# FFN of a two-layer encoder: gate and up as 2x2 blocks with seven products, down as a stretch of its own

## The chip, the cores and the metric

The kernel runs on one core of a Trainium2 chip. The metric is device microseconds of one launch. PE is TensorE's matmul engine and PEld its weight load, DVE is VectorE, ACT is ScalarE, POOL is GpSimd, SP is SyncE, which issues most DMAs. A bank is one of the eight PSUM banks of 128 x 512 f32.

## The reference

Two layers over 1024 tokens of 1024 features, everything in f32. The change touches the third line of a layer:

```
x = x + w_out( concat_g RMSNorm_g(out_g) )      # mixing: attention, gating, conv
h = RMSNorm(x);  gu = h @ w_gate_up             # 1024 -> 2 x 2816
x = x + (silu(gate) * up) @ w_down              # 2816 -> 1024
x = x + (p @ w_ple_proj) * sigmoid(RMSNorm(x) @ w_ple_gate)   # "PLE"
```

`D_FF` is 2816, so gate and up have 22 feature tiles of 128 each. RMSNorm's factor per token can be put in after a product, since it scales a whole token.

## The kernel before

Tokens stand on the free axis. The 1024 tokens are two halves of 512 (`hf` 0 and 1), the features eight tiles of 128 (`m`). A product of one 128 x 128 weight tile with 512 tokens is three matmuls (`step_mm`, L220 to L224): weights and tokens are each split into a rounded part and its remainder, high by high, high by low and low by high. The rounded part is a copy on ACT (`copy_h`), the remainder a subtraction on DVE (`sub_l`). `load_w` loads 128 x 1024 weights (512 KB) and splits them with one such copy (`wh`) and one subtraction (`wl`).

After mixing, `wo_first` and `wo_second(hf)` add w_out's product to X; `norm_add` makes the split form `hl` of X times the gain and sums its square on ACT and POOL; `norm_end` makes the factor per token (a power on POOL, L265) and spreads it (`bc`). Half 0 is ready earlier than half 1, since attention of the second half still runs as a background job (`bg.tick`), so the FFN begins with feature tiles 0 to 3 on half 0 alone (AHEAD, BEHIND) and gives half 1 its share of them at the end.

`gate_up(fi)` makes eight products for gate and eight for up of each half, the evacuation multiplying by `bc` (L1114), silu on ACT (L1115), another factor on POOL (L1116), gate times up on DVE (L1121), and then the split form `act` (L123, L126). `down(fs, acts)` takes the split activations of two feature tiles, for each of the eight output tiles and each half, and adds the bank into X on DVE (L1140). It runs one group behind gate and up (`pend`, `flush`), so a bank is evacuated while the next products run. After the last group `norm_add` forms the PLE's `hl`, and `ple(hf)` follows.

The code is written in this order, and a scheduler of the framework, working from its own times, fixes at build time the order of the instructions of each engine. Each engine then takes its queue strictly in that order; semaphores do the rest. Split forms live in 38 buffers of 4 KB (`U`), temporaries in six (`T`), weights in three buffers each of `raw`, `wh` and `wl`, PSUM in pools of three (`BA`), four (`BT`) and one bank (`BO`).

Of the kernel before, what the change touches and what calls it, by code (L numbers as in the profile page):

```python
# [12 lines left out]
ALU = mybir.AluOpType  # L13
# [59 lines left out]
def tile_encoder_trunk(ctx: ExitStack, tc: tile.TileContext, x, p, positions, norm_mix_g, w_in,  # L73
# [128 lines left out]


# [252 lines left out]
    for layer in range(DEPTH):  # L456
# [622 lines left out]
        def wo_second(hf):  # L1079
            xps = [U("X").rearrange("p (m s) -> p m s", m=2) for _ in range(4)]  # L1080
            for mp in range(4):
                nc.scalar.dma_start(out=xps[mp], in_=xd[2 * mp:2 * mp + 2, :, HALF[hf]]
                                    .rearrange("m p s -> p m s"))
            for mp in range(4):
# [3 lines left out]
                for m in (2 * mp, 2 * mp + 1):  # L1088
# [7 lines left out]
                    norm_add(nrm[hf], xo, "ffn", layer)  # L1096
# [3 lines left out]
        nx = [None, None]  # L1100

        def gate_up(fi, halves, bank, eng):
            acts, s = {}, {}

            def ff_unit(c0, evac):
                wh, wl = load_w(rows_of(w_gate_up[layer], 0, NK, c0, P), (NK, P), eng, eng and nc.vector)
                for hf in halves:
                    half_mm(bank, [((wh[:, k, :], wl[:, k, :]), nrm[hf].hl[k]) for k in range(NK)],
                            lambda b: evac(hf, b))

            def ev_gate(hf, b):
                t = s[hf] = T("sg")
                bc = nrm[hf].bc
                nc.vector.tensor_tensor(out=t, in0=b, in1=bc, op=ALU.mult)  # L1114
                nc.scalar.activation(t, t, AF.Silu)  # L1115
                nc.gpsimd.tensor_tensor(out=t, in0=t, in1=bc, op=ALU.mult)  # L1116

            def ev_up(hf, b):
                t = s[hf]
                a = acts[hf] = U("act", F32R)  # L1120
                nc.vector.tensor_tensor(out=t, in0=b, in1=t, op=ALU.mult)  # L1121
                copy_h(a[:, 0:512], t)
                sub_l(a[:, 512:1024], t, a[:, 0:512])

            ff_unit(fi * P, ev_gate)
            ff_unit(DFF + fi * P, ev_up)
            return acts

        def down(fs, acts, halves, bank, eng, last):
            ws = [load_w(rows_of(w_down[layer], fi * P, 1, 0, D), (1, D), eng, eng and nc.vector)  # L1130
                  for fi in fs]
            for hf in last:
                nx[hf] = Norm()
            for m in range(NK):
                cs = slice(m * P, (m + 1) * P)
                for hf in halves:
                    xo = X[hf][m]

                    def ev(b):
                        nc.vector.tensor_tensor(out=xo, in0=b, in1=xo, op=ALU.add)  # L1140

                    half_mm(bank, [((wh[:, 0, cs], wl[:, 0, cs]), a[hf])
                                   for (wh, wl), a in zip(ws, acts)], ev)
                    if hf in last:
                        norm_add(nx[hf], xo, "ple", layer)

        pend = []

        def ffn(fs, halves, bank=BU, eng=None, last=()):
            acts = [gate_up(fi, halves, bank, eng) for fi in fs]  # L1150
            flush()
            pend.append((fs, acts, halves, bank, eng, last))
# [133 lines left out]
```

## Time and profile before

| | us |
|---|---|
| median of 3 runs | 2527.86 (2526.82 to 2532.4) |
| the profiled execution | 2526.26 |
| its span | 2524.5 |
| PE busy | 2419.4 |
| DVE busy | 1367.7 |
| ACT busy | 799.9 |
| POOL busy | 572.4 |

The span is what the profile shows of one execution; 1.76 us of the profiled execution lie outside of it. The granted clock, averaged over the span, was 0.984 of full speed. The windows 500 to 1100 us and 1750 to 2300 us lie within the two layers' FFNs; a layer's PLE begins behind 1157 us and 2400 us. A row's last part in square brackets is the time that the engine stood idle before the instruction, and what released it.

### The profile page before, as it was taken

How to read it: one execution, taken by the hardware profiler on the slowest of the kernel's cores; microseconds unless marked ns; L12 is line 12 of the kernel's file. 1: busy time of each engine (PE TensorE's matmuls, PEld its weight loads, DVE VectorE, ACT ScalarE, POOL GpSimd, SP SyncE). 2: the span in 40 equal slices, each digit the busy share in tenths (PEclk: the TensorE clock that was granted, in tenths of full speed). 3: DMA queues.
4: the chain of work that ended last, by engine and by line, in shares of the span. 5: the costliest groups of instructions: out<-in, count | busy, mean ns of one | idle time of the engine just before them, and what ended most of it. 6: DMA issues, size and time to landing. Idle time of an engine off the chain costs nothing. (4 is left out here: it accounts for less than half of the span.)

```text
span 2524.5 us, 29666 instructions
## 1 busy us (share of the span) xinstructions
PE 2419.4 (96%) x11932; PEld 2034.0 (81%) x11932; DVE 1367.7 (54%) x2111; ACT 799.9 (32%) x1392; POOL 572.4 (23%) x423
## 2 busy tenths in 40 slices
PE   8898989999999999999999898899999999999999
PEld 6797767888888888887889876678888888888877
DVE  6996676534434434466469666764433443435652
ACT  5246573221111111135423456613111111112432
POOL 4123417410000000023421233363100000001321
PEclk9898999999999999999999899999999999999999
DMA  6110512311111111124321122132111111112232
GB/s 212 30 52 14 173 34 80 113 59 50 43 50 51 50 50 43 59 75 130 113 63 39 34 90 94 58 109 76 58 43 50 50 51 50 42 51 67 84 113 71
DMA packets 210538, 175.19 MB, mean 69 GB/s; under 512 B 5940, under 2 KB 191888, under 8 KB 210400
## 3 DMA queue, kind: packets, MB, share of 16 engines
q1 hardware_dynamic: 203904, 163.60, 21.0%
q10 hardware_dynamic: 6016, 9.45, 1.1%
q8 instruction: 94, 1.54, 0.2%
q0 software_dynamic: 480, 0.24, 0.1%
q14 instruction: 44, 0.36, 0.0%
HBM read 152.29 MB, written 20.97 MB: 69 GB/s over the span
## 5 line engine op out<-in xcount | busy, mean ns | idle before, releaser
L123 ACT ACTIVATE wh<-raw 128x1024 fp32r<-128x1024 f32 x198 | 208.1, 1059 | 810.4 <-PE pa L223 451.2
L222 PE MATMUL pa<-hl,wh 128*128 128x512 f32 x1128 | 443.3, 395 | 7.8 <-ACT hl L123 4.5
L224 PE MATMUL pa<-hl,wl 128*128 128x512 f32 x1128 | 442.3, 392 | 2.7 <-POOL wl L214 2.5
L223 PE MATMUL pa<-hl,wh 128*128 128x512 f32 x1128 | 443.4, 393 | 1.0 <-DVE hl L129 0.8
L1116 POOL TENSOR_TENSOR sg<-sg,st 128x512 f32<-128x512 f32 x88 | 138.6, 1576 | 1090.0 <-ACT sg L1115 1090.0
L214 DVE TENSOR_TENSOR wl<-raw,wh 128x1024 fp32r<-128x1024 f32 x198 | 249.0, 1265 | 60.5 <-ACT wh L123 59.0
L224 PE MATMUL pt<-hl,wl 128*128 128x512 f32 x664 | 259.7, 391 | 4.4 <-DVE wl L214 4.4
L222 PE MATMUL pt<-hl,wh 128*128 128x512 f32 x664 | 259.5, 391 | 0.0
L223 PE MATMUL pt<-hl,wh 128*128 128x512 f32 x664 | 259.0, 390 | 0.0
L222 PEld LDWEIGHTS pa<-hl,wh 128*128 128x128 f32 x1128 | 213.3, 189 | 54.0 <-ACT hl L123 6.5
L224 PEld LDWEIGHTS pa<-hl,wl 128*128 128x128 f32 x1128 | 213.6, 189 | 48.0 <-POOL wl L214 2.8
L223 PEld LDWEIGHTS pa<-hl,wh 128*128 128x128 f32 x1128 | 213.8, 190 | 45.9 <-DVE hl L129 2.2
L1140 DVE TENSOR_TENSOR X<-pa,X 128x512 f32<-128x512 f32 x226 | 155.0, 690 | 110.9 <-PE pa L224 109.8
L602 PE MATMUL pa<-wh,hl 128*128 128x256 f32 x640 | 180.8, 288 | 16.4 <-ACT zkv L615 11.7
L604 PE MATMUL pa<-wl,hl 128*128 128x256 f32 x640 | 182.3, 287 | 0.7 <-DVE wl L214 0.7
L605 PE MATMUL pa<-wh,hl 128*128 128x256 f32 x640 | 181.3, 286 | 0.0
L222 PE MATMUL pa<-act,wh 128*128 128x512 f32 x426 | 166.2, 390 | 1.3 <-DVE X L1140 1.3
L223 PE MATMUL pa<-act,wh 128*128 128x512 f32 x426 | 165.8, 389 | 0.0
L224 PE MATMUL pa<-act,wl 128*128 128x512 f32 x426 | 165.3, 390 | 0.0
L259 POOL TENSOR_TENSOR st<-st,sq 128x512 f32<-128x512 f32 x82 | 122.4, 1493 | 155.6 <-ACT sq L258 130.0
L488 DVE SCALAR_TENSOR_TENSOR acc<-glu,cols,acc 128x1009 f32<-128x1009 f32 (+14 forms) x120 | 154.2, 1287 | 1.3
L224 PEld LDWEIGHTS pt<-hl,wl 128*128 128x128 f32 x664 | 125.0, 188 | 30.8 <-DVE wl L214 4.9
(273 smaller groups left out, 4353.5 us busy)
## 6 DMA issues: line engine op xcount, KB each, us to landing
raw<-in_w_gate_up_dram SPq DMA_DIRECT2D x104, 512.0 KB, 3.9
raw<-in_w_down_dram SPq DMA_DIRECT2D x52, 512.0 KB, 3.7
raw<-in_w_ple_gate_dram SPq DMA_DIRECT2D x32, 512.0 KB, 4.4
raw<-in_w_in_dram SPq DMA_DIRECT2D x28, 512.0 KB, 3.8
raw<-in_w_out_dram SPq DMA_DIRECT2D x24, 512.0 KB, 3.6
xr<-xd SPq DMA_DIRECT2D x16, 512.0 KB, 3.3
xd<-xr SPq DMA_DIRECT2D x16, 512.0 KB, 2.6
X<-xd ACTq DMA_DIRECT2D x16, 512.0 KB, 5.1
```

The costliest lines, as they stand in the source:

```text
L123: nc.scalar.activation(dst, src, AF.Copy, scale=scale)
L214: (eng or nc.vector).tensor_tensor(out=l, in0=raw, in1=f(h), op=ALU.subtract)
L222: nc.tensor.matmul(b, lhsT=wh, rhs=hl[:, 0:512], start=first, stop=False)
L223: nc.tensor.matmul(b, lhsT=wh, rhs=hl[:, 512:1024], start=False, stop=False)
L224: nc.tensor.matmul(b, lhsT=wl, rhs=hl[:, 0:512], start=False, stop=last)
L259: (eng or nc.gpsimd).tensor_tensor(out=n.s, in0=n.s, in1=sq, op=ALU.add)
L488: nc.vector.scalar_tensor_tensor(out=a[:, lo:hi], in0=glu[c][:, lo + d:hi + d], scalar=wcol(t), in1=a[:, lo:hi], op0=ALU.mult, op1=ALU.add)
L602: nc.tensor.matmul(o, lhsT=x_[:, th], rhs=wh, start=(kc + k == 0), stop=False)
L604: nc.tensor.matmul(o, lhsT=x_[:, th], rhs=wl, start=False, stop=False)
L605: nc.tensor.matmul(o, lhsT=x_[:, tl], rhs=wh, start=False, stop=(kc == 1 and k == 3))
L1116: nc.gpsimd.tensor_tensor(out=t, in0=t, in1=bc, op=ALU.mult)
L1140: nc.vector.tensor_tensor(out=xo, in0=b, in1=xo, op=ALU.add)
```

## The change

Gate and up are computed as a product of 2 x 2 blocks: feature tiles 2j and 2j + 1 by the two halves of the features k (0 to 3 and 4 to 7) by the two halves of the tokens. Seven block products give all four result blocks where eight were made.

`first(j)` makes two of the seven: the full product of feature tile 2j with half 0, whose first four k are one of the seven and all eight of which are the result block. It reads the bank once in the middle, after k = 3 (`s1`, stored to DRAM in `sum_d`), and once at the end, for gate and for up. It uses `hl` of half 0 as before; the activation goes to DRAM (`act_d`).

`token_forms(k)` makes the five token blocks of the other products from normalised X of both halves (four scaled X, two sums each on DVE and on POOL, then `split` for each form: one ACT copy, one DVE subtraction), for each of four k.

`rest(j)` makes the other five for gate (i = 0) and then for up (i = 1), 4 k each. It reads `s1` back, loads four weight blocks, combines them on POOL in four instructions, splits five weight blocks (`wform`), and adds the products in two ways: some in one bank, some by DVE at evacuation. silu stands at the end of gate. The results go to DRAM.

Down follows as its own stretch. For each half, eight banks stay open over 22 feature tiles; for each tile its weights are loaded (so twice in all) and the activation is read back and split. X is reloaded from `xd`, to which `wo_second` stores it, and gets the eight banks at the end; `norm_add` for the PLE follows, with half 0's `norm_end` in the middle of half 1's.

The core of the diff (what the additions replace is in the listing of the kernel before):

```diff
         def wo_second(hf):
...
-                    norm_add(nrm[hf], xo, "ffn", layer)
+                    if hf == 0:
+                        norm_add(nrm[hf], xo, "ffn", layer)
+                    else:
+                        add_square(nrm[hf], xo, m)
+                nc.sync.dma_start(out=xd[2 * mp:2 * mp + 2, :, HALF[hf]]
+                                  .rearrange("m p s -> p m s"), in_=xp)
...
+        def first(j):
+            hl0, bc = nrm[0].hl, nrm[0].bc
+            c0 = 2 * j * P
+            a = None
+            for i, off in enumerate((0, DFF)):
+                wh, wl = load_w(rows_of(w_gate_up[layer], 0, NK, off + c0, P), (NK, P),
+                                nc.gpsimd if ahead else None, nc.vector if ahead else None)
+                b = BA()
+                for k in range(NK):
+                    step_mm(b, (wh[:, k, :], wl[:, k, :]), hl0[k], k == 0, k % HK == HK - 1, True)
+                    if k == HK - 1:
+                        s1 = T("s1")
+                        nc.vector.tensor_tensor(out=s1, in0=b, in1=bc, op=ALU.mult)
+                        nc.sync.dma_start(out=sum_d[j][i], in_=s1)
+                    if k % 2 == 1:
+                        bg.tick()
+                if i == 0:
+                    a = T("sg")
+                    nc.vector.tensor_tensor(out=a, in0=b, in1=bc, op=ALU.mult)
+                    nc.scalar.activation(a, a, AF.Silu)
+                    nc.gpsimd.tensor_tensor(out=a, in0=a, in1=bc, op=ALU.mult)
+                else:
+                    nc.vector.tensor_tensor(out=a, in0=b, in1=a, op=ALU.mult)
+                    nc.sync.dma_start(out=act_d[2 * j][:, HALF[0]], in_=a)
+        def split(src, eng=None):
+            hl = U("tf", F32R)
+            copy_h(hl[:, 0:512], src)
+            sub_l(hl[:, 512:1024], src, hl[:, 0:512])
+            return hl
+        def token_forms(k):
+            for hf in range(2):
+                for m in (k, k + HK):
+                    normed(hf, m)
+            b11, b21, b12, b22 = X[0][k], X[0][k + HK], X[1][k], X[1][k + HK]
+            t1 = T("t1")
+            nc.vector.tensor_tensor(out=t1, in0=b12, in1=b11, op=ALU.subtract)
+            nc.gpsimd.tensor_tensor(out=b12, in0=b22, in1=b12, op=ALU.subtract)
+            nc.vector.tensor_tensor(out=b11, in0=b22, in1=t1, op=ALU.subtract)
+            forms[0][k] = split(b11)
+            forms[1][k] = split(b12)
+            nc.gpsimd.tensor_tensor(out=b21, in0=b21, in1=b11, op=ALU.subtract)
+            forms[2][k] = split(t1)
+            forms[3][k] = split(b21)
+            forms[4][k] = split(b22)
+        def rest(j):
...
+                def wform(src):
...
+                    copy_h(h, src)
+                    sub_l(l, src, h)
+                    return h, l
...
+                def out_of(dst, src, b):
+                    if i == 0:
+                        nc.vector.tensor_tensor(out=dst, in0=b, in1=src, op=ALU.add)
+                        nc.scalar.activation(dst, dst, AF.Silu)
+                    else:
+                        c = T("cu")
+                        nc.vector.tensor_tensor(out=c, in0=b, in1=src, op=ALU.add)
+                        nc.vector.tensor_tensor(out=dst, in0=c, in1=dst, op=ALU.mult)
+                bank = BT if i else BA
+                tt(out=s3, in0=a21, in1=a22, op=ALU.add)
...
+                bb, bd, bc_ = bank(), bank(), bank()
+                prod(bb, wform(a11), 0, True, True)
+                u2, g = T("u2"), T("g")
+                nc.vector.tensor_tensor(out=u2, in0=bb, in1=s1, op=ALU.add)
+                prod(bd, wform(a21), 1, True, True)
+                nc.vector.tensor_tensor(out=g, in0=bd, in1=u2, op=ALU.add)
+                prod(bc_, wform(s3), 2, True, True)
+                out_of(gb[:, 512:1024], g, bc_)
+                prod(bd, wform(a22), 3, False, True)
+                out_of(gb[:, 0:512], u2, bd)
+                prod(bc_, wform(a12), 4, False, True)
+                out_of(ga[:, 512:1024], u2, bc_)
...
+        for j in range(AHEAD):
+            first(j)
         bg.drain()
+        first(AHEAD)
         wo_second(1)
+        for k in range(HK):
+            token_forms(k)
+        for j in range(AHEAD + 1, AHEAD + 1 + BEHIND):
+            first(j)
+        for j in range(NP2):
+            rest(j)
+            if AHEAD + 1 + BEHIND + j < NP2:
+                first(AHEAD + 1 + BEHIND + j)
...
+        for hf in range(2):
...
+            banks = [BO()] + [BA() for _ in range(3)] + [BT() for _ in range(4)]
+            for fi in range(NF):
+                wh, wl = load_w(rows_of(w_down[layer], fi * P, 1, 0, D), (1, D))
+                t = T("ac")
+                nc.sync.dma_start(out=t, in_=act_d[fi][:, HALF[hf]])
+                a = split(t)
+                for m in range(NK):
+                    cs = slice(m * P, (m + 1) * P)
+                    step_mm(banks[m], (wh[:, 0, cs], wl[:, 0, cs]), a, fi == 0, fi == NF - 1)
```

The change moves the order of the engines' queues in three places that matter below. The first is DVE in the steady part of an FFN. Before, remainders of weights (`wl`) stand among the evacuations of the two halves' gate (`sg`, L1114) and up (L1121):

```order
L1114 TENSOR_TENSOR sg_921_5743<-pa_920_5718,st_323_2467 128x512
L1114 TENSOR_TENSOR sg_923_5772<-pt_922_5747,st_324_2468 128x512
L214 TENSOR_TENSOR wl_940_5906<-raw_938_5904,wh_939_5905 128x1024
L1121 TENSOR_TENSOR sg_921_5743<-pa_927_5782,sg_921_5743 128x512
L126 TENSOR_TENSOR act_928_5807<-sg_921_5743,act_928_5807 128x512
L1121 TENSOR_TENSOR sg_923_5772<-pa_929_5811,sg_923_5772 128x512
L214 TENSOR_TENSOR wl_947_5970<-raw_945_5968,wh_946_5969 128x1024
L126 TENSOR_TENSOR act_930_5836<-sg_923_5772,act_930_5836 128x512
L1114 TENSOR_TENSOR sg_935_5871<-pt_934_5846,st_323_2467 128x512
```

Now, from the last evacuation of a gate block (`ga`, L1208) to the end of the up block's first five:

```order
L1208 TENSOR_TENSOR ga_1165_7017<-pa_1173_7032,u2_1176_7049 128x512
L125 TENSOR_TENSOR wl_1190_7134<-rw_1183_7121,wh_1189_7133 128x512 x2
L125 TENSOR_TENSOR wl_1194_7168<-ws_1185_7125,wh_1193_7167 128x512
L125 TENSOR_TENSOR wl_1194_7168<-rw_1184_7122,wh_1193_7167 128x512
L125 TENSOR_TENSOR wl_1198_7204<-rw_1184_7122,wh_1197_7203 128x512
L1224 TENSOR_TENSOR u2_1191_7149<-pt_1186_7130,s1_1182_7119 128x512
L1226 TENSOR_TENSOR g_1192_7150<-pt_1187_7131,u2_1191_7149 128x512
L1212 TENSOR_TENSOR cu_1195_7183<-pt_1188_7132,g_1192_7150 128x512
```

All of the next block's remainders stand together right behind the block's last evacuation, where before one stood among the evacuations of other products. ACT at the same place, before:

```order
L1115 ACTIVATE sg_921_5743<-sg_921_5743 128x512
L123 ACTIVATE wh_939_5905<-raw_938_5904 128x1024
L1115 ACTIVATE sg_923_5772<-sg_923_5772 128x512
L123 ACTIVATE act_928_5807<-sg_921_5743 128x512
L123 ACTIVATE wh_946_5969<-raw_945_5968 128x1024
L123 ACTIVATE act_930_5836<-sg_923_5772 128x512
```

and now:

```order
L1209 ACTIVATE gb_1166_7018<-gb_1166_7018 128x512 x2
L1209 ACTIVATE ga_1165_7017<-ga_1165_7017 128x512
L122 ACTIVATE wh_1189_7133<-rw_1183_7121 128x512 x2
L122 ACTIVATE wh_1193_7167<-ws_1185_7125 128x512
L122 ACTIVATE wh_1193_7167<-rw_1184_7122 128x512
```

The copies `wh` of the next block's first two products stand behind silu of `ga`, which waits for DVE's evacuation of `ga`; before, copies and silus alternated, and the copy stood ahead of the units that it served.

The second place is DVE where half 1 of X is done and its normalisation ends (`ms`, L263 before, then L268). Before, with the forms `hl` of half 1 and the evacuations of the first gates:

```order
L129 SCALAR_TENSOR_TENSOR hl_762_4527<-X_728_4346,cols1_145,hl_762_4527 128x512
L214 TENSOR_TENSOR wl_787_4684<-raw_785_4682,wh_786_4683 128x1024
L263 TENSOR_SCALAR ms_766_4539<-po_764_4533 128x4
L1114 TENSOR_TENSOR sg_772_4579<-pt_771_4554,st_323_2467 128x512
L214 TENSOR_TENSOR wl_794_4748<-raw_792_4746,wh_793_4747 128x1024
L1121 TENSOR_TENSOR sg_772_4579<-pa_776_4589,sg_772_4579 128x512
L126 TENSOR_TENSOR act_777_4614<-sg_772_4579,act_777_4614 128x512
L1114 TENSOR_TENSOR sg_782_4649<-pt_781_4624,st_323_2467 128x512
L1114 TENSOR_TENSOR sg_784_4678<-pa_783_4653,st_324_2468 128x512
```

Now the same place, from the last two of the eight `normed` (L1153), with the sums of `token_forms` at L1163 and L1165, the middle read `s1` of a first product at L1131, and the first remainder of a token form at L125:

```order
L1153 SCALAR_TENSOR_TENSOR X_726_4430<-X_726_4430,cols1_189,st_324_2512 128x512
L1153 SCALAR_TENSOR_TENSOR X_728_4432<-X_728_4432,cols1_189,st_324_2512 128x512
L1163 TENSOR_TENSOR t1_760_4618<-X_725_4429,X_613_3787 128x512
L1163 TENSOR_TENSOR t1_766_4642<-X_725_4429,X_613_3787 128x512
L1163 TENSOR_TENSOR t1_772_4666<-X_726_4430,X_614_3788 128x512
L1163 TENSOR_TENSOR t1_778_4690<-X_726_4430,X_614_3788 128x512
L1131 TENSOR_TENSOR s1_788_4729<-pa_787_4716,st_323_2511 128x512
L1165 TENSOR_TENSOR X_613_3787<-X_727_4431,t1_760_4618 128x512
L1165 TENSOR_TENSOR X_613_3787<-X_727_4431,t1_766_4642 128x512
L1165 TENSOR_TENSOR X_614_3788<-X_728_4432,t1_772_4666 128x512
L1165 TENSOR_TENSOR X_614_3788<-X_728_4432,t1_778_4690 128x512
L125 TENSOR_TENSOR tf_761_4622<-X_613_3787,tf_761_4622 128x512
```

Twelve instructions of the token forms (eight scaled X, four sums) stand ahead of the first product's middle read; behind it come four sums and five remainders before the end of that product (`sg`, L1137).

The third place is SP's queue of DMA issues at the end of the FFN of the first layer. Before, the last feature tiles' weights and the PLE's inputs:

```order
L209 DMA raw_1289_8500<-in_w_gate_up_dram 128x8x128
L209 DMA raw_1294_8535<-in_w_gate_up_dram 128x8x128
L209 DMA raw_1299_8570<-in_w_down_dram 128x1024
L209 DMA raw_1302_8576<-in_w_down_dram 128x1024
L1183 DMA pin_1317_8650<-in_p_dram 128x4x256
L1183 DMA pin_1320_8666<-in_p_dram 128x4x256
L209 DMA raw_1323_8682<-in_w_down_dram 128x1024
L209 DMA raw_1326_8688<-in_w_down_dram 128x1024
```

Now, where down begins (`ac` is an activation read back, `X` the reload):

```order
L1291 DMA ac_1266_7501<-act0_97 128x512
L211 DMA raw_1263_7495<-in_w_down_dram 128x1024
L1291 DMA ac_1271_7536<-act1_98 128x512
L1291 DMA ac_1276_7571<-act2_99 128x512
L1233 DMA act20_117<-ga_1200_7224 128x512
L1291 DMA ac_1281_7606<-act3_100 128x512
L1291 DMA ac_1286_7641<-act4_101 128x512
L1285 DMA X_1251_7479<-xd_96 128x2x512
L1285 DMA X_1252_7480<-xd_96 128x2x512
L1285 DMA X_1253_7481<-xd_96 128x2x512
L1285 DMA X_1254_7482<-xd_96 128x2x512
L211 DMA raw_1268_7530<-in_w_down_dram 128x1024
```

The down weights of the second feature tile are now issued behind a store of the last results (`act20`), which waits for them, five reads and four loads of X.

## Rows read from the trace of the kernel before

**Rows 1.** The page: the span, and TensorE's share of it.
```profile
span 2524.5 us, 29666 instructions
PE 2419.4 (96%) x11932; PEld 2034.0 (81%) x11932; DVE 1367.7 (54%) x2111; ACT 799.9 (32%) x1392; POOL 572.4 (23%) x423
```

**Rows 2.** Windows of the two FFNs: PE, PEld, DVE, ACT, POOL, clock, DMA.
```profile
500.00:1100.00 600.00, 600.00 (x2649) 496.82 (x2648) 250.17 (x327) 111.74 (x146) 67.37 (x43) 1.00 0.17 51
1750.00:2300.00 550.00, 550.00 (x2428) 455.43 (x2427) 221.39 (x289) 93.06 (x120) 54.03 (x35) 1.00 0.17 49
```

**Rows 3.** Timeline in the first FFN: start, duration, engine, line, operation.
```profile
701.72 0.39 PE L224 MATMUL pa<-hl,wl 128*128 128x512 f32 x1
701.95 0.39 PE L222 MATMUL pt<-hl,wh 128*128 128x512 f32 x1
702.15 0.69 DVE L1114 TENSOR_TENSOR sg<-pa,st 128x512 f32<-128x512 f32 x1 [4.75 <-PE pa L224]
702.94 0.61 ACT L1115 ACTIVATE sg<-sg 128x512 f32<-128x512 f32 x1
703.06 1.23 DVE L214 TENSOR_TENSOR wl<-raw,wh 128x1024 fp32r<-128x1024 f32 x1 [0.23 <-ACT wh L123]
...
707.39 0.39 PE L222 MATMUL pa<-hl,wh 128*128 128x512 f32 x1
```

**Rows 4.** Groups by line and shape: busy us, mean ns of one, idle before.
```profile
L126 DVE TENSOR_TENSOR act<-sg,act 128x512 fp32r<-128x512 f32 x88 | 66.7, 758 | 29.3 <-ACT act L123 29.3
L126 DVE TENSOR_TENSOR pT<-pt,pT 128x512 fp32r<-128x512 f32 x96 | 64.4, 687 | 17.3 <-ACT pT L123 16.9
L123 ACT ACTIVATE wh<-raw 128x1024 fp32r<-128x1024 f32 x198 | 208.1, 1059 | 810.4 <-PE pa L223 451.2 <-PE pt L223 288.3 <-issue 30.1
L123 ACT ACTIVATE act<-sg 128x512 fp32r<-128x512 f32 x88 | 55.6, 632 | 197.2 <-DVE sg L1121 197.2
L123 ACT ACTIVATE hl<-X,cols 128x512 fp32r<-128x512 f32 x80 | 56.9, 718 | 135.7 <-DVE X L1093 74.2 <-POOL X L1245 36.4 <-DVE X L1140 24.9
L258 ACT ACTIVATE sq<-X 128x512 f32<-128x512 f32 x70 | 43.1, 618 | 22.7 <-DVE X L1093 13.8 <-POOL as L940 6.2 <-DVE X L1140 2.7
L265 POOL TENSOR_TENSOR rcol<-ms,mhalf 128x4 f32<-128x4 f32 x12 | 14.8, 1238 | 51.5 <-DVE ms L263 51.5
L1245 POOL TENSOR_TENSOR X<-sg,X 128x512 f32<-128x512 f32 x31 | 41.3, 1334 | 95.1 <-DVE sg L1238 95.1
```

**Rows 5.** Timeline after the first FFN: DVE beside POOL, and alone.
```profile
1150.03 8.09 POOL L259 TENSOR_TENSOR st<-st,sq 128x512 f32<-128x512 f32 x5 [24.29 <-ACT st L255]
...
1152.40 4.59 DVE L129 SCALAR_TENSOR_TENSOR hl<-X,cols,hl 128x512 fp32r<-128x512 f32 x3
...
1158.11 1.40 DVE L129 SCALAR_TENSOR_TENSOR hl<-X,cols,hl 128x512 fp32r<-128x512 f32 x2
```

**Rows 6.** Timeline: three waits of PE at a layer's PLE.
```profile
1161.77 0.80 PE L224 MATMUL pt<-hl,wl 128*128 128x512 f32 x1 [4.43 <-DVE wl L214]
...
2401.73 0.50 PE L222 MATMUL pa<-pT,pwh 128*128 128x512 f32 x1 [2.40 <-ACT pwh L123]
...
2414.61 0.77 PE L222 MATMUL pa<-hl,wh 128*128 128x512 f32 x1 [2.98 <-DVE sg L1238]
```

**Rows 7.** Windows of 5 us around those waits.
```profile
1160.00:1165.00 5.00, 3.23 (x8) 2.56 (x9) 5.00 (x5) 2.15 (x3) 2.77 (x2) 0.66 0.34 101
2400.00:2405.00 5.00, 3.08 (x12) 2.25 (x13) 5.00 (x4) 3.91 (x5) 4.06 (x3) 1.00 0.10 31
2410.00:2415.00 5.00, 2.02 (x9) 1.43 (x8) 2.43 (x5) 2.11 (x2) 1.05 (x2) 0.93 0.82 227
2415.00:2420.00 5.00, 5.00 (x19) 3.95 (x19) 2.90 (x3) 1.12 (x2) 2.51 (x2) 0.73 0.61 180
```

**Rows 8.** The busiest window's DMA rate, and issues to landing of down weights.
```profile
25.00:30.00 5.00, 4.98 (x24) 3.83 (x23) 4.97 (x7) 2.31 (x5) 2.07 (x2) 1.00 1.02 394
...
raw<-in_w_down_dram SPq DMA_DIRECT2D x52, 512.0 KB, 3.7
```

More of the change, by code (lines that the diff above doesn't have):

```diff
@@ L43 @@
 N_T = 6
-FG = 2
 PLE_LAG = 2
-N_AHEAD = 4
-AHEAD = ((0, 1), (2,))
-BEHIND = ((3,),)
+NP2 = NF // 2
+AHEAD = 4
+BEHIND = 3
 C1 = 1
@@ L201, in tile_encoder_trunk @@
     xd = dp.tile([NK, P, S], F32, name="xd")
+    act_d = [dp.tile([P, S], F32, name=f"act{i}") for i in range(NF)]
+    sum_d = [[dp.tile([P, 512], F32, name=f"sum{i}_{j}") for j in range(2)] for i in range(NP2)]
     def load_w(src, shape, eng=None, heng=None):
@@ L1095, in wo_second @@
                     half_mm(BA, [((wh[:, k, cs], wl[:, k, cs]), mhl[hf][k]) for k in range(4)], ev)
-                    norm_add(nrm[hf], xo, "ffn", layer)
-            norm_end(nrm[hf])
[L1100 to L1152, printed above, removed]
-        def flush():
-            if pend:
-                a = pend.pop()
-                down(*a)
-                for hf in a[-1]:
-                    norm_end(nx[hf], BO)
+                    if hf == 0:
+                        norm_add(nrm[hf], xo, "ffn", layer)
+                    else:
+                        add_square(nrm[hf], xo, m)
@@ new lines, in tile_encoder_trunk, with normed @@
+        forms = [[None] * HK for _ in range(5)]
+        def split(src, eng=None):
[3 more added lines that the diff above has]
+            return hl
+        def normed(hf, m):
+            nc.vector.scalar_tensor_tensor(out=X[hf][m], in0=X[hf][m], scalar=col("ffn", layer, m),
+                                           in1=nrm[hf].bc, op0=ALU.mult, op1=ALU.mult)
+        def token_forms(k):
[13 more added lines that the diff above has]
+            forms[4][k] = split(b22)
@@ L1161, in tile_encoder_trunk @@
+        xpair = [None, None]
+        ahead = True
         wo_first()
@@ L1203, in tile_encoder_trunk @@
             pw.append((ph, pl))
+        nx = [None, None]
+        for hf in range(2):
+            xps = [U("X").rearrange("p (m s) -> p m s", m=2) for _ in range(4)]
+            for mp in range(4):
+                nc.sync.dma_start(out=xps[mp], in_=xd[2 * mp:2 * mp + 2, :, HALF[hf]]
+                                  .rearrange("m p s -> p m s"))
+            banks = [BO()] + [BA() for _ in range(3)] + [BT() for _ in range(4)]
[7 more added lines that the diff above has]
+                    step_mm(banks[m], (wh[:, 0, cs], wl[:, 0, cs]), a, fi == 0, fi == NF - 1)
+            nx[hf] = Norm()
+            for m in range(NK):
+                xo = X[hf][m] = xps[m // 2][:, m % 2]
+                nc.vector.tensor_tensor(out=xo, in0=banks[m], in1=xo, op=ALU.add)
+                if hf and m == 0:
+                    norm_end(nx[0], BO)
+                norm_add(nx[hf], xo, "ple", layer)
         last = layer == DEPTH - 1
@@ L1252, in ple @@
                 norm_end(nrm[hf], BO)
-        for hf in range(2):
-            ple(hf)
+        ple(0)
+        norm_end(nx[1], BO)
+        ple(1)
 _INS = ['x', 'p', 'positions', 'norm_mix_g', 'w_in', 'q_norm_g', 'k_norm_g', 'sink', 'gm_ln_g',
```

56 lines of the change are left out of this document (41 added, 15 removed).

## The prediction

> **What bounds the kernel now.** I began with the page: PE is busy 2419.4 of 2524.5 us [rows 1]. An average hides stages, so windows of the two FFNs came next: PE is busy 600.00 of 600 us and 550.00 of 550, DVE 250 and 221, at a granted clock of 1.00 (2.4 GHz) and about 50 GB/s [rows 2]. In an FFN nothing is waited for, so every matmul taken away is time gained and every new wait is time lost, in full. The timeline gives the pace: from 701.95 to 707.39 begin 24 matmuls, 5.44 us, or 0.227 each (a record's 0.39 overlaps the next one) [rows 3]. The same rows show why no evacuation is felt: PE goes on at 701.95 in another bank while DVE reads the old one at 702.15.
>
> **The matmuls.** Gate and up of a layer were 44 weight tiles x 8 k x 2 halves x 3 = 2112 matmuls. Now `first` makes 11 x 2 x 8 x 3 = 528 and `rest` 11 x 2 x 5 x 4 x 3 = 1320: 264 fewer, 59.9 us per layer, 119.7 in all. Down's count stays.
>
> **Boundaries between blocks.** Within `rest` each block's weight forms stand behind the last evacuation of the block before. From gate to up, counted from the start of the last matmul: 0.43 until DVE begins (701.72 to 702.15), evacuation 0.69, 0.10, silu 0.61 [rows 3], two copies of 512 at 0.63 [rows 4] (PE's first wait is for the second), 0.05 to PE: 3.14, less the usual 0.23, is 2.9 us. 11 of them are 32.1 per layer. From up to gate no silu stands between; PE gets four matmuls (0.91) that need copies alone, then waits for 0.43 + 0.69, the product with silu 0.69, two remainders at 0.72 (between 0.687 and 0.758 [rows 4]) and 0.05: 3.30, less the 1.13 that five matmuls take anyway, is 2.2. There are ten, of which a `first` covers three: 7 x 2.2 = 15.2. Together 47 (low 38: 2.5 and 1.5 each; high 52, if DVE is also slowed by POOL's weight sums). Within a block products in three banks cover the evacuations, 12 matmuls (2.7 us) to each, so these cost nothing; if that cover went, each of the 5 evacuations would show its 0.69. The two weight loads and the `s1` of a block are issued a block ahead (60 matmuls, 13.6 us), and POOL's four weight sums (5.3 at 1.33) end within it.
>
> **Token forms.** DVE does, in a row, 8 scaled X at 0.70 (1158.11) [rows 5], 8 sums at 0.69, 20 remainders at 0.72, 3 `wl` at 1.23 [rows 3] and 11 evacuations at 0.69: 36.9 us. The power of the normalisation adds 1.24 [rows 4]. POOL makes 8 sums of 1.33 meanwhile, 10.6 us; beside POOL a DVE instruction with two SBUF inputs took 4.59/3 = 1.53 where alone it took 0.70 [rows 5], so 0.54 us is lost per us of POOL, at most 5.8; I take 5. That is 43 us against 96 matmuls of `first`, 21.8 us: PE idles 21 (15, if half 1's early part hides behind w_out; 28, if POOL's power comes late). The Trainium skill ("SBUF — State Buffer", section "Who interferes with whom") says that such a DVE instruction and a reading GpSimd one exclude each other for a whole instruction; by it the loss would be up to 10.6 and the idle time 27; the rows agree in kind but show half the loss.
>
> **The smaller terms, per layer.** Ahead of the attention's end, the second product's middle read stands behind 8 scaled X of half 0 (5.6), a weight copy (1.2 by the DVE row of 1024) and two evacuations (1.4); 12 matmuls (2.7) cover: 5.5, and `bc` 1.5 late: 7 (4 if background work fills PE; 13 if the scaled X run beside POOL at 1.53). The three `first` among the `rest` have their middle read behind a gate evacuation, 1.6 each (0.43 + 2 x 0.69 - 0.23): 4.8 (0; 6). Where down starts, ACT has pT 0.63, two PLE weights and one down weight at 1.06 and a token form 0.63 to do [rows 4]: 4.4 idle. The second tile's weights stand behind the store of the last result: evacuation and product 1.8, then 3.1 MB of reads at 394 GB/s [rows 8] 8.0, 2.4 for landing (3.7 less 1.3 of transfer [rows 8]), copy 1.06: 13.3, against 4.4 + 5.4: 3.5 more, so 7.9 (5; 13). Between the halves of down all eight banks are evacuated and ACT has eight copies and eight squares, 8 x (0.72 + 0.62) = 10.7 [rows 4], ahead of the first activation's split, with one evacuation 1.1 before it: 12 (9; 15). The waits at the PLE's start (4.43; 2.40 and 2.98 [rows 6], with their slow clock) go, since half 0's forms are ready a half of down earlier: -6 (-7; 0). The adds into X on DVE (L1140) fall to 16 per layer, but lay beside PE and give nothing. Stores and reads through DRAM lie beside PE too: in down a tile needs 0.52 + 0.26 MB in 5.44 us, 145 GB/s, against windows of 394 [rows 8]. Without this cover see the third rival.
>
> **Clock.** After the waits of 4.43 and 2.98 us the clock was 0.66, then 0.93 and 0.73 [rows 6, 7]: each time 3.4 us at 1.2 GHz, so 1.7 lost; after that of 2.40 it stayed at 1.00. Some six waits per layer above 3 us (token forms, down's start, its middle): 10 (3 with two; 42 with 25).
>
> **Sum.** 47 + 21 + 7 + 4.8 + 7.9 + 12 - 6 + 10 = 104 per layer, 208 for both, less 119.7: +88 on the profiled execution's 2526.3 (1.6 below the median of the runs shown): 2615 us. All low ends give 67 x 2 - 120 = +14 (2541), all high ends 169 x 2 - 120 = +218 (2744).
>
> **Rivals.** First, not slower: the waits are shorter than their queues say. The point is 59.9 us per layer. If boundaries cost 1.2 us each (18 x 1.2 = 21.6), as when ACT and DVE are ahead of PE at most of them, and the other terms lie at their low ends (29, clock included), a layer loses 51 and the time is 2526 + 101 - 120 = 2508. DVE at 42% in FFNs [rows 2] speaks for it; against it, that queues are taken in order and the forms stand right behind the evacuation. Chance 0.15: 0.11 faster, 0.04 the same.
> Second, clock: the 2.9 us of a boundary lie beside the wait of 2.98, after which it fell [rows 6, 7]. If it falls at all 22, at 1.7 each, that is +37: 2652; if two stretches join each time, +75: 2690. The wait of 2.40 without a fall, and full speed between waits 14 us apart, speak against it. Chance 0.14. The Trainium skill ("TensorE: Matmul & The Clock Gate", section "A second HAM failure mode: psum-queue depth-cycling") tells of a kernel that cycled through PSUM banks, whose short idle times between groups made the clock swing; here both kinds of gap occur, so it raises this chance but doesn't settle it.
> Third, down becomes bound by DMA: with twice the weights and activations in rows of 2 KB, at the 101 GB/s of one window [rows 7] a tile would take 7.8 us, 2.3 more, x 88 = +206: 2821. It decides from 145 GB/s; that 101 was no limit (share 0.34) speaks against. Chance 0.04.
> Fourth, the change doesn't do what its count says: if a saved matmul gave back its record of 0.39 us [rows 3], 528 would give 206, and the time would be 2529. The pace speaks against. Chance 0.03, counted as the same.
>
> **How the numbers follow.** The forecast, 2615 us, has 0.64. The range, 2545 to 2690, holds it nearly whole and most of the clock's case, and leaves out the first, third and fourth rivals, 0.2 in all. This kernel's measurement tells 0.2% (5 us) from no change. Faster has 0.11; the same 0.04 + 0.03 = 0.07; slower 0.64 + 0.14 + 0.04 = 0.82.
>
> **What would show it.** Right: 528 fewer matmuls by count; PE idle about 2.9 us, released by ACT `wh`, before the first matmul of each up block, and 2.2 by DVE `wl` before gate blocks; some 20 us of PE's idle time at the middle reads, released by DVE `s1`; in down 5.44 us per tile with PE full; waits by ACT at its start and middle. Wrong: PE full across boundaries, or waits there below 1.5 us (first rival); windows of `rest` with a granted clock well below 1.00 (second); down's matmuls released by DMA or by ACT `wh` waiting for `raw` (third). Waits of the queues longer than worked out, or others that I don't name, would put the time above the range.

## The result, and the profile after

The changed kernel takes 2666.9 us (median of four runs, 2659.98 to 2668.87) against 2527.3 before: a ratio of 1.055 (95% interval 1.052 to 1.057), 139.6 us slower. The forecast was 2615 us, +88, range 2545 to 2690: the direction and the range held, the size was 52 us short.

The page of the kernel after, its span, its busy line and the granted clock by slices of 67 us, in tenths:

```profile
span 2665.9 us, 30234 instructions
PE 2387.9 (90%) x11404; PEld 1972.8 (74%) x11404; DVE 1453.5 (55%) x2241; ACT 905.5 (34%) x1610; POOL 744.6 (28%) x551
...
PEclk9999998899999989899999999898999999999999
```

528 matmuls are gone, as counted, and PE's busy time is 31.5 us less [rows 1], but the span is 141.4 us more, and the clock is below 9 tenths in six slices (three before). Windows of the kernel after (columns as in [rows 2]): the first layer's blocks behind its last `first`, its first half of down, and two neighbouring stretches of 5 us within the blocks:

```profile
704.00:958.00 254.00, 225.12 (x916) 178.16 (x916) 122.04 (x176) 54.74 (x98) 78.01 (x56) 0.95 0.28 94
975.00:1091.00 116.00, 115.86 (x504) 95.69 (x504) 41.79 (x46) 36.29 (x46) 0.66 (x1) 0.99 0.42 143
730.00:735.00 5.00, 3.96 (x18) 2.96 (x16) 1.38 (x2) 0.91 (x2) 3.18 (x3) 1.00 0.00 1
735.00:740.00 5.00, 3.55 (x10) 2.86 (x11) 3.10 (x5) 2.96 (x6) 0.00 (x0) 0.74 0.01 3
```

Where PE was busy 600 of 600 us [rows 2] it is now idle for 29 of 254, at a clock of 0.95. Down's own stretch is full: 504 matmuls in 116.0 us are 0.230 each, so DMA at 143 GB/s doesn't bound it. The last two rows lie on either side of a block boundary: full clock before it, 0.74 behind it. The timeline of that boundary, gate to up:

```profile
733.57 0.39 PE L228 MATMUL pa<-tf,wl 128*128 128x512 f32 x1
...
734.00 0.69 DVE L1208 TENSOR_TENSOR ga<-pa,u 128x512 f32<-128x512 f32 x1 [2.03 <-PE pa L228]
...
734.73 0.63 ACT L1209 ACTIVATE ga<-ga 128x512 f32<-128x512 f32 x1 [2.09 <-DVE ga L1208]
735.26 1.13 ACT L122 ACTIVATE wh<-rw 128x512 fp32r<-128x512 f32 x2
735.91 1.29 DVE L125 TENSOR_TENSOR wl<-rw,wh 128x512 fp32r<-128x512 f32 x2 [1.21 <-ACT wh L122]
...
736.45 0.50 PE L224 MATMUL pt<-tf,wh 128*128 128x512 f32 x1 [2.49 <-ACT wh L122]
```

This is the chain that was worked out: the last matmul begins at 733.57, DVE's evacuation 0.43 later, silu of `ga` behind it, only then the copies `wh`, and PE goes on 2.88 after that last matmul, 2.65 more than its pace. The first matmul's record is longer (0.50), and a stretch at 1.2 GHz follows. The waits of PE in the window 704 to 958 (us in total, times, longest):

```profile
PE pt L224 <- ACT wh L122: 19.9, 8, 2.5
PE pa L224 <- ACT wh L122: 6.6, 7, 0.9
PE pa L228 <- DVE wl L125: 4.6, 7, 0.7
```

Eight waits of 2.5 us at gate to up, and at the seven boundaries from up to gate two short ones of 0.94 and 0.66. Token forms, timeline (DVE and PE):

```profile
497.43 5.39 DVE L1153 SCALAR_TENSOR_TENSOR X<-X,cols,st 128x512 f32<-128x512 f32 x8 [2.46 <-ACT st L298]
502.74 2.49 DVE L1163 TENSOR_TENSOR t<-X,X 128x512 f32<-128x512 f32 x4
...
505.75 6.21 DVE L1165 TENSOR_TENSOR X<-X,t 128x512 f32<-128x512 f32 x4
505.89 0.80 PE L224 MATMUL pa<-hl,wh 128*128 128x512 f32 x1 [9.11 <-DVE s L1131]
...
511.89 3.42 DVE L125 TENSOR_TENSOR tf<-X,tf 128x512 fp32r<-128x512 f32 x2
...
521.12 0.79 PE L224 MATMUL pa<-hl,wh 128*128 128x512 f32 x1 [10.89 <-DVE s L1131]
```

PE's middle read stands behind eight scaled X (5.39) and four sums (2.49), as the order showed, and the next wait, 10.89, behind sums and remainders. The sum took 6.21/4 = 1.55 each beside POOL, where [rows 5] gave 0.70 alone; over these instructions some 7.5 us are lost to it. POOL's eight sums took 14.65 us there, not the 10.6 of the working, so DVE lost 0.51 us per us of POOL, close to the 0.54 of [rows 5]. By the rule of the Trainium skill ("SBUF — State Buffer", section "Who interferes with whom"), that the two exclude each other, the loss could be up to all of the 14.65, an estimate; the trace shows half of it. Down's start and middle, timeline:

```profile
961.31 3.56 SPq L1285 DMA_DIRECT2D X<-xd  x4
...
963.47 1.06 ACT L122 ACTIVATE wh<-raw 128x1024 fp32r<-128x1024 f32 x1 [2.79 <-DMA raw<-in_w_down_dram]
...
965.10 0.79 PE L224 MATMUL po<-tf,wh 128*128 128x512 f32 x1 [6.94 <-ACT tf L122]
965.23 1.65 SPq L211 DMA_DIRECT2D raw<-in_w_down_dram  x3
...
974.03 1.06 ACT L122 ACTIVATE wh<-raw 128x1024 fp32r<-128x1024 f32 x1 [6.22 <-DMA raw<-in_w_down_dram]
...
975.14 0.50 PE L224 MATMUL po<-tf,wh 128*128 128x512 f32 x1 [2.23 <-ACT wh L122]
...
1100.12 0.79 PE L224 MATMUL po<-tf,wh 128*128 128x512 f32 x1 [8.83 <-ACT tf L122]
```

Both waits are there: 6.94 behind ACT's PLE copies and the first weights (ACT itself waits 2.79 us for their load, which the forecast left out), then 2.23 for the second tile's weights, which are issued behind the reload of X (961.31) and land for a copy at 974.03; and 8.83 between the halves.

### The profile page after: what moved, and what is told of

It reads as the page before. It is cut to its first block, busy times and chain, and to the rows that moved or that the text cites. A ratio compares the mean times of both kernels' runs of the same rounds, so it can differ in the third digit from the quotient of the medians.

```text
span 2665.9 us, 30234 instructions
## 1 busy us (share of the span) xinstructions
PE 2387.9 (90%) x11404; PEld 1972.8 (74%) x11404; DVE 1453.5 (55%) x2241; ACT 905.5 (34%) x1610; POOL 744.6 (28%) x551
## 3 DMA queue, kind: packets, MB, share of 16 engines
q8 instruction: 90, 1.47, 0.2%
## 5 line engine op out<-in xcount | busy, mean ns | idle before, releaser
L224 PE MATMUL pt<-tf,wh 128*128 128x512 f32 x792 | 326.5, 415 | 54.7 <-ACT wh L122 54.7
L226 PE MATMUL pt<-tf,wh 128*128 128x512 f32 x792 | 323.3, 408 | 0.0
L224 PE MATMUL pa<-hl,wh 128*128 128x512 f32 x648 | 264.4, 409 | 62.9 <-DVE s L1131 52.9
L228 PE MATMUL pt<-tf,wl 128*128 128x512 f32 x792 | 315.4, 404 | 0.0
L224 PE MATMUL pa<-tf,wh 128*128 128x512 f32 x704 | 280.0, 400 | 19.5 <-ACT wh L122 19.5
L228 PE MATMUL pa<-tf,wl 128*128 128x512 f32 x704 | 273.1, 394 | 9.2 <-DVE wl L125 9.2
L226 PE MATMUL pa<-tf,wh 128*128 128x512 f32 x704 | 277.0, 394 | 0.0
L228 PE MATMUL pa<-hl,wl 128*128 128x512 f32 x648 | 259.1, 404 | 4.5 <-POOL wl L216 3.3
L226 PE MATMUL pa<-hl,wh 128*128 128x512 f32 x648 | 262.1, 405 | 1.0 <-DVE hl L128 0.8
L224 PEld LDWEIGHTS pt<-tf,wh 128*128 128x128 f32 x792 | 159.4, 201 | 98.4 <-ACT wh L122 64.0
L224 PEld LDWEIGHTS pa<-hl,wh 128*128 128x128 f32 x648 | 125.8, 194 | 99.6 <-DVE s L1131 59.3
L226 PEld LDWEIGHTS pt<-tf,wh 128*128 128x128 f32 x792 | 157.6, 199 | 33.9
L228 PEld LDWEIGHTS pt<-tf,wl 128*128 128x128 f32 x792 | 156.3, 197 | 34.2
L224 PEld LDWEIGHTS pa<-tf,wh 128*128 128x128 f32 x704 | 134.9, 192 | 55.7 <-ACT wh L122 28.8
```

## The account in three terms

Each kernel's span against that of before is compared with three terms: the difference in matmuls at 0.227; PE's idle time between records, with 0.17 more for each wait (a record of 0.39 reaches that far past the pace); and the clock, half of the time at 1.2 GHz in which PE was not idle. In us:

| kernel | matmuls | idle | clock | sum | span |
|---|---|---|---|---|---|
| after | -119.7 | +188.2 | +66.2 | +134.6 | +141.4 |
| fill | -64.8 | +181.8 | +55.6 | +172.6 | +179.4 |
| fill2 | -64.8 | +129.7 | +42.2 | +107.0 | +116.9 |
| early | -119.7 | +156.9 | +57.4 | +94.6 | +95.8 |
| early2 | -119.7 | +94.0 | +27.7 | +2.1 | +2.8 |
| inter | -119.7 | +158.6 | +58.7 | +97.6 | +103.0 |
| combo1 | -119.7 | +54.2 | +25.0 | -40.5 | -41.3 |
| combo2 | -119.7 | +20.6 | +9.4 | -89.7 | -87.5 |
| downonly | 0 | +21.7 | +10.1 | +31.8 | +30.0 |
| down2 | 0 | +5.0 | +4.4 | +9.4 | +8.2 |

The terms account for every kernel within 10 us, most within 3; what makes up the 7 us left over in the kernel after and the 10 in fill2 isn't known. For the kernel after, the time at 1.2 GHz is 256 us (83 before), in 49 stretches (15).

The clock's term has a part that the edits don't touch: in the first 400 us, ahead of the first FFN, the time at 1.2 GHz was 34 us in the kernel before, 27 in the kernel after and 44 in fill2. So the blocks are taken by themselves as well (552 to 958 and 1870 to 2276 us of the kernel after): there 22 stretches of 3.4 us cost 37.1 us of the 66.2, in the same blocks of fill2 it was 5.1, of early 20.8, of early2 none.

## The experiments

All start from the changed kernel, but for downonly and down2, which start from the kernel before; that one was timed beside each (medians of 2525.3 to 2527.6 us).

**fill: work put into the wait, first try.** After the last product of a gate block (FILL is 11):

```diff
-                prod(bc_, wform(a12), 4, False, True)
+                w12 = wform(a12)
+                prod(bc_, w12, 4, False, True)
+                if i == 0:
+                    spare = BO()
+                    for q in range(FILL):
+                        nc.tensor.matmul(spare, lhsT=w12[0][:, q % HK, :],
+                                         rhs=forms[4][q % HK][:, 0:512], start=q == 0,
+                                         stop=q == FILL - 1)
```

> Edit: behind the last product of each gate block, 11 more matmuls (2.5 us) are put into PE's queue, into a spare bank that nothing reads; they fall into the wait for the up block's weight copies. Theory (each of the 22 waits of 2.48 us costs 2.65 us and then a slow stretch of the clock of 3.4 us, 1.7 us of work): the waits stay as long as they are, PE is busy in them, the clock stays at 2.4 GHz, and the time falls by about 20 x 1.7 = 34 us, from 2667 to about 2633, although 242 matmuls were added. Rival A (the clock falls for another reason, as DMA or the mean load of the stretch): no slow stretch goes, time within 5 us of 2667. Rival B (the added matmuls delay the next block): up to 242 x 0.227 = 55 us slower, 2720.

2707.0 us, ratio 1.071 (1.069 to 1.074): 40 slower than the changed kernel. The scheduler, which owns the order, put the matmuls (L1237) ahead of the last two products, presumably since their bank was free early. Timeline at a boundary:

```profile
739.90 2.66 PE L1237 MATMUL po<-tf,wh 128*128 128x512 f32 x11
...
745.32 0.69 DVE L1209 TENSOR_TENSOR gb<-pa,u 128x512 f32<-128x512 f32 x1 [4.52 <-PE pa L229]
...
750.48 0.50 PE L225 MATMUL pt<-tf,wh 128*128 128x512 f32 x1 [2.48 <-ACT wh L123]
```

DVE waits 4.52 for the fourth product, 2.5 more than the 2.03 of the kernel after, and the wait behind the block is still 2.48. The matmuls added 55 us of work and took up none of the waits. It is rival B's sign, but not its mechanism, and doesn't settle what the waits cost in clock, so it was repeated.

**fill2: work put into the wait, in its place.** The same matmuls into the bank whose evacuation lies just ahead of the last product:

```diff
-                prod(bc_, wform(a12), 4, False, True)
+                a12w = wform(a12)
+                prod(bc_, a12w, 4, False, True)
+                if i == 0:
+                    for q in range(11):
+                        nc.tensor.matmul(bd, lhsT=a12w[0][:, q % HK, :],
+                                         rhs=forms[4][q % HK][:, 0:512], start=q == 0,
+                                         stop=q == 10, skip_group_check=True)
                 out_of(ga[:, 512:1024], u2, bc_)
```

> Edit: as in the run named fill, 11 more matmuls for each gate block, but into the bank whose evacuation lies just before the last product, so that they stand in PE's queue directly behind the last product and ahead of the up block's first. Theory (each of the 22 waits of 2.48 us costs its length and then a slow stretch of 3.4 us at half clock): the matmuls lie in the wait, PE idles there for under 0.3 us, nearly all of the some 20 slow stretches behind these waits go, and the time falls by 25 to 35 us, to about 2637. Rival A (the slow stretches have another cause than the waits): the time stays within 5 us of 2667. Rival B (the added matmuls delay the block behind them): slower, up to 2720.

2639.4 us, 27.5 faster than the changed kernel with 242 matmuls more; ratio to before 1.045 (1.043 to 1.047). Timeline at a boundary:

```profile
737.51 2.65 PE L1235 MATMUL pa<-tf,wh 128*128 128x512 f32 x11
...
738.43 0.63 ACT L1209 ACTIVATE ga<-ga 128x512 f32<-128x512 f32 x1 [2.09 <-DVE ga L1208]
738.97 1.14 ACT L122 ACTIVATE wh<-rw 128x512 fp32r<-128x512 f32 x2
...
740.16 0.50 PE L224 MATMUL pt<-tf,wh 128*128 128x512 f32 x1
```

silu and the copies come at the same distance as before, but PE works through the wait and takes up the next block with no idle time. The idle term falls by 58.5, the matmuls add 54.9, and the clock term falls by 24.0, in spite of the 7 us more that this execution lost in its first 400 us. A window of the same blocks as 704 to 958 of the kernel after, where the clock was 0.95:

```profile
703.00:943.00 240.00, 228.85 (x969) 181.83 (x968) 118.65 (x170) 55.16 (x98) 78.05 (x56) 0.99 0.29 96
```

In the blocks of both layers the clock's cost falls from 37.1 to 5.1 us. So the waits themselves cost a slow clock, 32 us over 22 boundaries; rival A falls.

**early2: weight forms ahead of the evacuations.** The block is cut into stages, and the next block's are written between those of the present one (here and below, remarks behind # are not in the code):

```diff
+            for n, (j, i) in enumerate(seq):
+                at(n, 4)        # first product, third product's weight form
+                at(n + 1, 2)    # next block: POOL's sums
+                at(n + 2, 1)    # the one after it: weight loads
+                at(n, 5)        # second and third product, last two weight forms
+                at(n + 1, 3)    # next block: its first two weight forms
+                at(n, 6)        # fourth and fifth product, last evacuations
```

> Edit: the weight loads, POOL sums, copies and remainders of a block are written ahead of the block before's last evacuations (copies then stand before silu on ACT, remainders before the last evacuation on DVE), except where a first lies between. Theory (the waits at 15 + 14 boundaries inside the rest come from the forms queued behind the evacuations, and the clock falls after the waits): idle time of about 2.65 x 16 + 1.95 x 14 = 70 us goes, and with it some 16 to 20 slow stretches at 1.7 = 27 to 34: 2667 - 100 = about 2567. Rival A (the waits are set by POOL's sums or the weight loads, which land late): waits of 1 to 2.5 us stay at half the boundaries, 2610 to 2640. Rival B (what is saved comes back as contention of DVE and POOL or as later waits): above 2640.

2528.9 us (ratio 1.0012, 1.0002 to 1.0023): 138 faster than the changed kernel, level with the kernel before. Blocks of the first layer behind the last `first`, window:

```profile
703.00:893.00 190.00, 190.00 (x844) 157.39 (x843) 133.07 (x160) 52.91 (x90) 82.73 (x52) 1.00 0.33 110
```

PE is busy 190.00 of 190 us at a clock of 1.00. The idle term fell by 94 (70 expected, which counts 16 of the 22 waits at gate to up; all 22 went, and with them the sum is 86) and the clock by 38. The waits were queue order, not POOL or DMA: DVE (133 of 190 us) and POOL (83) carry the same work and nothing waits for it.

**early: a milder form.** The next block's loads and POOL sums are written early, but its first two weight forms only ahead of the last evacuation:

```diff
+                next(cur)        # fourth and fifth product
+                if nxt:
+                    next(nxt)    # next block: its first two weight forms
+                next(cur)        # last evacuation
```

> Edit: a milder form of early2: loads and POOL sums of a block are written after the third product of the block before and its first two weight forms before that block's last evacuation. In the engines' queues this moves the forms only at the boundaries from up to gate; from gate to up the copies still stand behind silu and the remainders behind the evacuation. Theory: the waits of 0.95 and 0.66 us (1.95 with the usual pace) at 14 boundaries go, the 22 waits of 2.48 and their slow stretches stay: 2667 - 27 - 3 = about 2637. Rival (early2 gained by loads and POOL sums that come earlier, not by the place in the queues): most of early2's gain is here too, below 2600.

2616.2 us (ratio 1.035, 1.033 to 1.038). The up to gate waits are gone and the 22 of 2.48 us stayed, as the theory has it, though loads and sums are written a block ahead here too: the place in the queues is what counts. The idle term fell by 31 and the clock by 9 (in the blocks by 16), so the gain was 51 where 30 was expected. Two of its gate to up boundaries, timeline, and the windows around them:

```profile
740.42 0.79 PE L224 MATMUL pt<-tf,wh 128*128 128x512 f32 x1 [2.48 <-ACT wh L122]
...
771.83 0.50 PE L224 MATMUL pt<-tf,wh 128*128 128x512 f32 x1 [2.48 <-ACT wh L122]
```

```profile
737.00:742.00 5.00, 2.52 (x9) 1.73 (x8) 2.81 (x5) 3.23 (x6) 2.33 (x3) 0.81 0.19 52
769.00:774.00 5.00, 2.52 (x11) 1.80 (x10) 3.40 (x6) 3.23 (x6) 2.28 (x3) 1.00 0.16 54
```

The same wait of 2.48 us is followed by a slow stretch in one and not in the other. There was one behind 20 of the 22 in the kernel after, 12 in fill, 13 here and 20 in inter.

**inter: token forms spread among more cover.**

```diff
-BEHIND = 3
+BEHIND = 6
...
+        todo = list(range(AHEAD + 1, AHEAD + 1 + BEHIND))
         for k in range(HK):
+            first(todo.pop(0))
             token_forms(k)
-        for j in range(AHEAD + 1, AHEAD + 1 + BEHIND):
+        for j in todo:
             first(j)
```

> Edit: six first instead of three run beside the token forms, alternating with them in the program, and none among the rest. Theory (PE's 20 us of idle time there is DVE's in-order work of 43 us against 21.8 us of cover, and each first among the rest costs 2.1 us at its two middle reads): cover doubles, idle time falls by 10 to 15 us per layer, the first's waits among the rest go (3 x 2.1), three boundaries lose their cover (3 x 1.95): about -10 to -15 idle and -3 clock per layer, 2667 - 30 = about 2637. Rival (the wait is the order itself: the eight scaled X and four sums stand ahead of the first middle read whatever runs beside): no change, 2660 to 2672.

2627.6 us (ratio 1.040, 1.037 to 1.043): 39 faster. The long waits of PE in the same place, and DVE ahead of the first, timeline:

```profile
501.10 6.43 DVE L1153 SCALAR_TENSOR_TENSOR X<-X,cols,st 128x512 f32<-128x512 f32 x8
507.45 0.68 DVE L1163 TENSOR_TENSOR t<-X,X 128x512 f32<-128x512 f32 x1
508.05 0.68 DVE L1131 TENSOR_TENSOR s<-pa,st 128x512 f32<-128x512 f32 x1
...
508.79 0.79 PE L224 MATMUL pa<-hl,wh 128*128 128x512 f32 x1 [3.33 <-DVE s L1131]
...
521.03 0.50 PE L228 MATMUL pa<-hl,wl 128*128 128x512 f32 x1 [1.79 <-DVE wl L216]
```

In place of 9.11 and 10.89 stand 3.33 and 1.79, the second for a weight remainder. That is less DVE work uncovered, as the theory has it, but the edit moved DVE's order too: one sum stands between the scaled X and the middle read where four stood, and the other sums and remainders are spread. How much is due to the added matmuls and how much to the order isn't shown.

**downonly: the new down with the old gate and up.** In place of `first`, `token_forms` and `rest`:

```diff
+        for fi in range(4, NF):
+            gate_up(fi, (0, 1))      # eight products each, as before; result to act_d
```

> Edit: down as in the changed kernel (own stretch, eight banks, activations through DRAM, weights twice), but gate and up as 16 products for each pair of tiles as in the kernel before, so no token forms, no blocks and no saved matmuls. Theory (from the trace after: down's start 9.2 idle and 3.4 of clock, its middle 9 and 4, less the waits at the PLE of the kernel before, 6 to 7): about +18 per layer, 2527 + 36 = about 2563. Rival A (down's stretch also loses by contention or DMA in its steady part): above 2590. Rival B (the start's wait belongs to the blocks before it, not to down): below 2545.

2555.9 us (ratio 1.012, 1.010 to 1.014), +28 on before where 36 was expected. PE's waits from 430 to 1200 us:

```profile
PE po L224 <- ACT tf L122: 14.8, 2, 8.4
PE po L226 <- DVE tf L125: 1.2, 1, 1.2
```

Down's start and middle are two waits, 14.8 us together in this layer; its steady part adds none.

**combo1: early2 and inter.** Edits as above.

> Edit: early2 and inter together. Theory (the terms are independent: boundaries 138 and token forms with the first's middle reads 39): 2667 - 138 - 39 = about 2490. With the first all ahead of the rest, all 36 boundaries are of early2's kind. Rival (the same waits are counted in both, or the weight forms now collide with the token forms' end): 2505 to 2529.

2477.4 us (ratio 0.980, 0.978 to 0.982): 190 below the changed kernel, where 177 was expected. The two gains add, with some 12 us more that weren't traced, and every boundary of `rest` is now of early2's kind. Against the kernel before it is 2.0% faster.

**combo2: combo1 with down's start and middle mended.**

```diff
+                if n == len(seq) - 2:
+                    ple_inputs()
...
+                if fi == 6:
+                    x_reload(hf)
+                if hf and 2 <= fi < 2 + NK:
+                    norm_add(nx[0], X[0][fi - 2], "ple", layer)
...
+            if hf == 0:
+                down_in(1, 0)
+                down_in(1, 1)
```

> Edit: combo1, and down's start and middle rewritten: the PLE's inputs are made before the last two blocks, X is reloaded after the seventh feature tile, the second half's first two weight and activation forms are made ahead of the eight evacuations, and half 0's norm sums lie among the second half's tiles. Theory (down's start costs 7.7 us and a slow stretch of 6.8, its middle 9.6 and 6.8 to 13.7, per layer): 7.7 + 3.4 + 8 + 5 = about 22 per layer is won, 2490 - 44 = about 2446. Rival (the waits move: to the last blocks that get the PLE's inputs, or to the evacuations of the banks that the next half needs at once): 2470 to 2490.

2437.5 us (ratio 0.964, 0.962 to 0.966): 40 below combo1, and 3.6% below the kernel before. Windows of its first layer, the blocks, down's start, and down with its middle:

```profile
575.00:855.00 280.00, 280.00 (x1241) 231.86 (x1241) 202.30 (x238) 81.86 (x138) 133.37 (x84) 1.00 0.36 120
855.00:860.00 5.00, 3.58 (x17) 2.67 (x16) 5.00 (x7) 0.79 (x2) 0.00 (x0) 1.00 0.71 207
860.00:1100.00 240.00, 240.00 (x1061) 198.72 (x1060) 103.14 (x117) 82.84 (x109) 11.84 (x7) 1.00 0.49 164
```

One wait of 1.42 us is left from 575 us to the PLE; ahead of that the token forms and the first block's weights still hold PE up (3.28, 1.82 and 3.34 us).

**down2: the mended down with the old gate and up.** downonly with combo2's edits; `ple_inputs` stands before the last two `gate_up`.

> Edit: downonly with down's start and middle rewritten as in combo2, so gate and up have their 16 products for each pair of tiles and down is the mended stretch. Theory (the mended stretch wins what it won between combo1 and combo2, 40 us, and combo2's lead over the kernel before is the 528 saved matmuls less the token forms' waits): 2556 - 40 = about 2516, and combo2 stays some 75 to 85 us ahead of this kernel. Rival (combo2's lead comes mostly from the new down, not from the block products): 2470 or below.

2534.5 us (ratio 1.003, 1.002 to 1.004), 18 above what was expected. The mend won 21, not 40: the PLE's inputs found a new wait. Timeline at the end of gate and up:

```profile
890.56 1.06 ACT L122 ACTIVATE pwh<-praw 128x1024 fp32r<-128x1024 f32 x1 [1.56 <-DMA praw<-in_w_ple_proj_dram]
892.31 1.06 ACT L122 ACTIVATE wh<-raw 128x1024 fp32r<-128x1024 f32 x1 [0.69 <-DMA raw<-in_w_gate_up_dram]
...
893.42 0.80 PE L224 MATMUL pa<-hl,wh 128*128 128x512 f32 x1 [6.16 <-ACT wh L122]
```

ACT's queue takes the copy of a PLE weight (890.56, waiting for its load) ahead of the next gate's weights, so PE stands 6.16 us (6.79 in the second layer). In combo2 the same inputs fall among blocks whose weight forms are a block ahead. combo2's lead over down2 is 97 us, of which some 13 are these two new waits of down2: the rest comes from the 528 matmuls, not from down.

## Why the prediction was right, and where it was short

Term by term, per layer (us, waits of the first layer with 0.17 for each; the clock is half of the whole):

| term | forecast | measured |
|---|---|---|
| matmuls | -59.9 | -59.9 |
| boundaries | 47 | 11 x 2.65 + 7 x (0.95 + 0.66 + 0.34) = 42.8 |
| token forms | 21 | 9.11 + 10.89 + 1.10 + 0.81 + 0.7 = 22.6 |
| ahead of attention's end | 7 | 1.47 + 1.01 + 0.34 = 2.8 |
| `first` beside the rest (four, not three) | 4.8 | 4 x (1.38 + 0.79 + 0.34) = 10.0 |
| down's start | 7.9 | 6.94 + 2.23 + 0.34 = 9.5 |
| down's middle | 12 | 8.83 + 0.78 + 0.34 = 10.0 |
| the PLE's start | -6 | -4.6, and 1.34 + 1.40 + 0.34 for new waits behind it: -1.5 |
| clock | 10 | 66.2 / 2 = 33 |

The waits came to 96 in this layer and by the account to 94 per layer, where the forecast's rows give 94. That the sums agree so well is luck, since misses of up to 5 us cancel: boundaries, attention's end and down's middle were taken too long, the `first` too short and the PLE's gain too large. Reading in-order queues against durations of the trace was right to some 5 us per place, and early2, inter and combo2 show that these waits, with the clock behind them, are what the loss was: with most of them gone the change is worth -87.

The step that was mis-sized is "**Clock.** [...] Some six waits per layer above 3 us", 20 us for both layers against 66.2. The count was wrong because the border was drawn between the rows of 2.40, without a fall, and 2.98, with one [rows 6, 7]. The boundaries' waits of 2.48 lie on the near side of it and still had a fall behind 20 of 22. Their blocks cost 37.1 us in clock where the forecast has nothing. The places that it did count (token forms, down's start and middle) cost 25.5 in all, near its 20: their slow stretches are longer than 3.4 us (mostly 6.8 to 13.7), but lie in part in the waits. The end of attention adds 4.4. Some 7 us of the 52 are those that the account leaves over.

The trace of the kernel before already held a shorter wait with a fall behind it, near 406 us, ahead of the attention's end, and the prediction doesn't weigh it:

```profile
405.79 0.96 PE L222 MATMUL pa<-hl,wh 128*128 128x512 f32 x3 [2.15 <-ACT hl L123]
```

```profile
405.00:410.00 5.00, 4.01 (x15) 3.24 (x16) 5.00 (x7) 5.00 (x9) 1.82 (x2) 0.72 0.00 0
```

So length alone gave no border between 2.40 and 2.98, even by the rows at hand. The second rival, which let the clock fall at all 22, had both the mechanism and the price: 37 forecast, 37.1 in the blocks. It was given 0.14. The Trainium skill ("TensorE: Matmul & The Clock Gate", section "A second HAM failure mode: psum-queue depth-cycling") tells of a kernel whose clock swung with short idle times between groups of matmuls. The blocks agree with it: 20 of 22 waits of 2.48 us had 3.4 us at 1.2 GHz behind them.

The first rival (waits shorter than the queues say) did not come: they were as long. The third (DMA) did not: down ran at pace. The fourth (the saving not as counted) is excluded by the account, in which 0.227 per matmul closes for all kernels, and by combo2's lead of 97 us over down2, where by that rival's price the 528 matmuls would have given 206.

## What to carry to other kernels

Where one engine is full, price a change by the queue positions of what feeds it: write down what stands behind the last evacuation of a block, and add the durations. Forms that need only loads should be written a block ahead, which here was worth about what the change cost (138 of 139.6 us). A wait can have a second price in the clock: go through all waits of the trace with the clock behind each, not three of them, and for a wait that the kernel before never shows in series, take both cases into the sum.

## What the runs showed of the hardware

- Waits of equal length (2.48 us) had a slow stretch of 3.4 us behind them in 20, 12, 13 and 20 of 22 cases in four kernels. The eight waits of 1.38 us in the kernel after had none. What decides it is not settled by these runs.
- 242 matmuls more made the kernel 27.5 us faster (fill2): work that nobody reads, in place of a wait, paid for itself by the clock (37.1 us of cost in the blocks, 5.1 with it).
- DVE instructions with two SBUF inputs lost 0.51 us per us of POOL's sums beside them in the kernel after (7.5 of 14.65 us).
